# Retention state of the prompt multiplied between the output projection and the gate product, in a one-layer hybrid decoder on one core

## The chip, the cores and the metric

One core of a Trainium2 chip runs the whole step as one program. The time is what the device needs for one execution, in microseconds (us); the median of several executions is given, with the lowest and the highest beside it. The profile is of one further execution. Its engines are named as in its rows: PE is TensorE's matmuls and PEld its weight loads, DVE is VectorE, ACT is ScalarE, POOL is GpSimd, SP is SyncE, which only issues DMAs here.

## What is computed

A decoder layer with two kinds of mixer heads (SSD and retention) and a SwiGLU feed-forward part, on 264 columns that matter at the end: 256 prompt tokens and 8 sample tokens (16 meta tokens run ahead of the prompt, so 272 prompt columns pass through the mixers). Cut to what the change touches:

```python
h = h + rmsnorm(mix @ w_out, post_mix_g)          # the kernel's stage "o" and its norm
f = rmsnorm(h, pre_ffn_g)                         # the second norm of the same h
f = (silu(f @ w_gate) * (f @ w_up)) @ w_down      # stages "f" and "d"
h = h + rmsnorm(f, post_ffn_g)
# two of the states of the prompt that are outputs too:
ret_state  = sum over tokens j of  gamma**(271 - j) * outer(k_j, v_j)      # per head, 256 x 256, 4 heads
ssm_state  = sum over tokens j of  w_j * outer(x_j * dt_j, B_j)            # per group
```

The two state sums need nothing of `w_out` or of the feed-forward part: their operands (`ktok`, `vtok`; `xdt`, `btok`) are there long before, and nothing reads them but the stores to the outputs.

## The kernel before

All activations lie transposed: 128 features on the partitions, the tokens along the free axis. A matrix of 2048 rows is 16 k-tiles. Weights are not resident: `Stream` (line 110) walks through all weight blocks in the order of use, eight 128x128 blocks to a chunk of 512 KB. Each chunk is loaded by SP into `raw` (four buffers), cast by ScalarE to a rounded copy `hi` (line 123) and subtracted by VectorE to the remainder `lo` (line 124); `hi` and `lo` have three buffers each. Every 128x128 block then takes three matmuls (`three`, lines 132 to 134): `hi` by the rounded activation, `hi` by its remainder, `lo` by the rounded activation. An activation is split in the same manner by `split` (line 653): ScalarE writes the rounded half (line 654), VectorE the remainder (line 655).

`gemm` (line 136) goes through output tiles one after the other, each with all its k-tiles, and evicts each tile from its PSUM bank. With `outer=n` the first n output tiles run k-outer: for each k-tile all n tiles are advanced, so that the product can begin when the first k-tile of its input is there. For stage `f` (gate and up, 88 output tiles) this holds for the first six (OUTF = 6): 16 k-tiles x 6 tiles x 3 = 288 matmuls, which use 12 chunks of weights. Their first four banks are of the pool `pg` (4 banks, tag `g`), the other two of `pm` (4 banks, tag `m`), in which the norm's sums (`n30`, `n40`), the banks of the state products (`ps0` to `ps7`, `hs0`, `hs1`) are allocated too.

Between stage `o` and stage `f` lies the double norm (lines 777 to 802). `rstds` multiplies the sums of squares by ones on TensorE and takes Ln and Exp on ScalarE (lines 645, 647). Then, for each of the 16 k-tiles: VectorE multiplies by `rstd` (line 788) and adds the residual `xr` (line 789), `split` makes `fh` and `fl` (ScalarE, then VectorE), ScalarE squares the tile into `hq` (line 792), and GpSimd adds that to a running sum `hs` (line 797). The residual comes in pairs of tiles, by DMAs that GpSimd issues (line 786) into three buffers of the pool `sd`; the result is stored for later, four tiles at a time, into `hd` (line 802), also from GpSimd's queue. The second norm's factor `rhc` is wanted only when the first six tiles of `f` are evicted: `ffn_norm` (line 806) runs after the k-outer part of `gemm`, before its evictions (line 859).

`do_pret` (line 619) is the retention state: for each of 8 (head, half) tiles three matmuls of 256 columns into a bank, a copy by ScalarE (`pso`, line 628) and a store issued by GpSimd. `PRE = 1`: head 0 stands behind the norm's loop, heads 1 to 3 after the first six tiles of `f`, followed by `do_pssm` (line 430), which weighs `xdt` on VectorE (line 432) and multiplies it into `hs0` and `hs1`.

The order on each engine is fixed when the program is built: a planner takes, for each engine, the first ready instruction in program order, with some moved up: the chunk casts by 1500 places, an eviction's first reading by 3000. Tiles of one pool and tag are handed buffers; the pool `sp` (tag `s`) has 27 slots of 128x1120 words, in which `o`, `mh`, `ml`, `fh`, `fl`, `ktok`, `vtok`, `xdt`, `btok` and later `ah`, `al` lie.

Of the kernel before, what the change touches and what calls it, by code (L numbers as in the profile page):

```python
# [7 lines left out]
F32 = mybir.dt.float32  # L8
F32R = mybir.dt.float32r
AF = mybir.ActivationFunctionType  # L10
# [5 lines left out]
P = 128  # L16
DM = 2048
KT = DM // P
NMETA = 16
NPR = 272  # L20
NA = 280
NO = 264
# [24 lines left out]
DECAY_ACT = False  # L47
WARM = 9
OUTF = 6
PRE = 1  # L50


@with_exitstack
def hybrid_step(ctx: ExitStack, tc: tile.TileContext, wall, xT, pp, cc, dmask, cs, convst, ssm, ret,
                yT, oconv, opssm, opret, osssm, osret):
    nc = tc.nc
    V, A, G, T = nc.vector, nc.scalar, nc.gpsimd, nc.tensor
    MULT, ADD, SUB, MAX, MIN = ALU.mult, ALU.add, ALU.subtract, ALU.max, ALU.min

    cp = ctx.enter_context(tc.tile_pool(name="cp", bufs=1))  # L60
    st = ctx.enter_context(tc.tile_pool(name="st", bufs=3))
    sp = ctx.enter_context(tc.tile_pool(name="sp", bufs=NSLOT))
    ta = ctx.enter_context(tc.tile_pool(name="ta", bufs=9))
    sd = ctx.enter_context(tc.tile_pool(name="sd", bufs=3))
# [6 lines left out]
    def slot(name, w=NA, n=4, dt=F32):  # L71
        return sp.tile([P, n, w], dt, name=name, tag="s")

    def small(name, w=NA):
        t = ta.tile([P, 308], F32, name=name, tag="t")
        return t[:, :w]

    def bank(name, w=512):
        t = pm.tile([P, 512], F32, name=name, tag="m")
        return t[:, :w]  # L80

    def table(name):
        return tc.keep_in_program_order(A.preload_act_table_set(name))

    def load(out, in_):
        G.dma_start(out, in_)
# [6 lines left out]
    def par(n, i=0, w=1):  # L93
        return pps[:, PP[n][0] + i:PP[n][0] + i + w]
# [41 lines left out]
    def gemm(name, xin, nk, n, m0, m1, evict, outer=0, pool=pg, before=None):  # L136
        off = 0
        if outer:
            pss = [pg.tile([P, 512], F32, name=f"{name}{m}", tag="g") if m < m0 + 4 else
                   pm.tile([P, 512], F32, name=f"{name}{m}", tag="m") for m in range(m0, m0 + outer)]  # L140
            for k in range(nk):
                xh, xl = xin(k, n)
                for ps in pss:
                    three(ps[:, :n], xh, xl, k == 0, k == nk - 1)
            if before:
                before()
            for m in range(m0, m0 + outer):
                evict(m, pss[m - m0][:, :n])
            m0 += outer
        for m in range(m0, m1):  # L150
            ps = pool.tile([P, 512], F32, name=f"{name}{m}", tag="g" if pool is pg else "m")
            for k in range(nk):
                xh, xl = xin(k, n)
                three(ps[:, :n], xh, xl, k == 0, k == nk - 1)
            evict(m, ps[:, :n])
# [271 lines left out]
                                   ps, MULT, ADD)  # L427
            yield

    def do_pssm():  # L430
        for b in range(3):
            V.tensor_tensor(xdt[b], xdt[b], wj[:, b, :].unsqueeze(2).to_broadcast([P, 16, 64]), MULT)
        for g in range(2):
            ps = bank(f"hs{g}")
            for b in range(3):
                T.matmul(ps, btok[:, b, g * P:(g + 1) * P], xdt[b][:, 8 * g:8 * g + 8, :].rearrange("p h d -> p (h d)"),
                         start=(b == 0), stop=(b == 2))
            for f in (0, 256):
                t = small(f"hso{g}{f}", 256)
                A.copy(t, ps[:, f:f + 256])  # L440
                load(opssm[:, g * 512 + f:g * 512 + f + 256], t)
# [177 lines left out]
    def do_pret(h0, h1):  # L619
        for h in range(h0, h1):  # L620
            for t in range(2):
                m = 2 * h + t
                ps = bank(f"ps{m}", 256)
                for b in range(3):
                    T.matmul(ps, ktok[b][:, m, :], vtok[b][:, 2 * h:2 * h + 2, :].rearrange("p a d -> p (a d)"),
                             start=(b == 0), stop=(b == 2))
                o = small(f"pso{m}", 256)
                A.copy(o, ps)
                load(opret[:, m, :], o)


    def rstds(name, groups, scale, outs=None, load_table=True):
        pss = []
        for g, sums in enumerate(groups):
            ps = bank(f"{name}{g}", NO)
            for i, s in enumerate(sums):
                T.matmul(ps, ones, s, start=(i == 0), stop=(i == len(sums) - 1))
            pss.append(ps)
        if load_table:
            table("natural_log_exp_and_others")  # L640
        rs = outs or [small(f"{name}r{g}", NO) for g in range(len(groups))]
        sc = scale if isinstance(scale, list) else [scale] * len(groups)
        with tc.high_priority(offset=1000):
            for ps, r, c in zip(pss, rs, sc):
                A.activation(r, ps, AF.Ln, bias=eps, scale=c)
            for r in rs:
                A.activation(r, r, AF.Exp, scale=-0.5)
        return rs
# [4 lines left out]
    def split(hi, lo, src, scale):  # L653
        A.activation(hi, src, AF.Copy, scale=scale)  # L654
        V.scalar_tensor_tensor(lo, src, scale, hi.bitcast(F32), MULT, SUB)
# [98 lines left out]
    def ev_norm(o, gain):  # L754
        st_ = {}

        def ev(m, ps):
            i, j = divmod(m, 4)
            sq = small(f"{gain}q{m}", NO)
            with tc.high_priority(offset=3000):  # L760
                A.activation(sq, ps, AF.Square)
                V.tensor_scalar(o[i][:, j, :], ps, par(gain, m), None, MULT)
            if m == 0:
                st_["a"] = sq
            elif m < KT - 1:
                n = small(f"{gain}s{m}", NO)
                G.tensor_tensor(n, st_["a"], sq, ADD)
                st_["a"] = n
            else:
                st_["b"] = sq  # L770
        return ev, st_

    o = [slot(f"o{i}", NO) for i in range(4)]
    ev, sums = ev_norm(o, "g_post")
    table("natural_log_exp_and_others")
    gemm("o", min_, KT, NO, 0, KT, ev, outer=4)
# [1 line left out]
    hd = dp.tile([P, KT, NO], F32, name="hd")  # L778
    fh = [slot(f"fh{i}", NO, dt=F32R) for i in range(4)]
    fl = [slot(f"fl{i}", NO, dt=F32R) for i in range(4)]  # L780
    ha = None
    for k in range(KT):
        i, j = divmod(k, 4)
        if k % 2 == 0:
            xr = sd.tile([P, 2, NO], F32, name=f"xr{k}", tag="st")
            load(xr, xT[:, k:k + 2, NMETA:NA])
        ok = o[i][:, j, :]
        V.tensor_tensor(ok, ok, rstd, MULT)
        V.tensor_tensor(ok, ok, xr[:, k % 2, :], ADD)
        split(fh[i][:, j, :], fl[i][:, j, :], ok, par("g_ffn", k))  # L790
        sq = small(f"hq{k}", NO)
        A.activation(sq, ok, AF.Square)
        if k == 0:
            ha = sq
        elif k < KT - 1:
            n = small(f"hs{k}", NO)
            G.tensor_tensor(n, ha, sq, ADD)
            ha = n
        else:
            hb = sq  # L800
        if j == 3:
            load(hd[:, 4 * i:4 * i + 4, :], o[i])
    do_pret(0, PRE)
    rhc = cp.tile([P, NO], F32, name="rhc")

    def ffn_norm():
        rstds("n4", [[ha, hb]], 1.0 / DM, [rhc], False)


    mix.close()  # L810
# [44 lines left out]
    def ev_f(m2, ps):  # L855
# [12 lines left out]
        if m < 41 and (m + 1) * 25 // 41 > n:  # L868
            pace = ta.tile([P, 1], F32, name=f"pace{m}", tag="pace", bufs=2)
            tc.keep_in_program_order(G.tensor_copy(pace, t[:, 0:1]))  # L870
            state_step(n)

    gemm("f", fin, KT, NO, 0, OUTF, ev_f, outer=OUTF, before=ffn_norm)
    do_pret(PRE, 4)
    do_pssm()
    gemm("f", fin, KT, NO, OUTF, 2 * FT, ev_f)

# [22 lines left out]
    for n in range(8):  # L900
        ok = o2[n // 2][:, 2 * (n % 2):2 * (n % 2) + 2, :]
# [116 lines left out]
```

## Time and profile before

| | us |
|---|---|
| median of 3 runs | 1285.83 |
| lowest to highest | 1283.55 to 1287.29 |
| the profiled execution | 1283.67 |
| its span, first to last instruction | 1281.8 |

| stage | stretch of the span, us |
|---|---|
| norm, mixers and their projections | 0 to 379 |
| `o`: the output projection | 379 to 472.2 |
| double norm, then the six k-outer tiles of `f` | 472.2 to 516.8 |
| rest of the state products | 517 to 531.4 |
| rest of `f` | 531.4 to 1007 |
| `d`: the down projection | 1007 to 1264 |
| last norm and output | 1264 to 1281.8 |

Matmuls are pipelined: a row's duration of 0.28 us is that from start to end, and the next one starts 0.12 us after it. A loss on TensorE is therefore read from start to start. A wide fp32 matmul (the state products, the sums by ones) shows as two instructions.

### The profile page before, as it was taken

The numbers are of one execution on the slowest core, as the hardware profiler recorded it, in microseconds if no ns is written. First come the engines' busy times: TensorE is split into PE (matmuls) and PEld (weight loads), VectorE is DVE, ScalarE is ACT, GpSimd is POOL, SyncE is SP. The second block draws the span as 40 slices with busy tenths as digits, with TensorE's granted clock in tenths as the row PEclk, the third lists the DMA queues.
The fourth block names the chain that finished last, engine by engine and source line by source line (L and its number), as shares of the span: only waits on it lengthen the run. The fifth ranks groups of instructions, "written<-read, shape, count | busy, mean of one in ns | idle before, by whom it ended". The sixth has DMA issues, their size and how long they took to land.

```text
span 1281.8 us, 24583 instructions
## 1 busy us (share of the span) xinstructions
PE 1255.2 (98%) x10078; PEld 1240.1 (97%) x10078; DVE 825.6 (64%) x1259; ACT 608.0 (47%) x838; POOL 170.0 (13%) x236
## 2 busy tenths in 40 slices
PE   8999999999999999999999999999999999999994
PEld 7999999999999998899999999999999999999994
DVE  7978879884774459466666666666666544444445
ACT  6665344455854446444444444444444433333331
POOL 3320001110001225201110110101101000000013
PEclk9999999999999999999999999999999999999997
DMA  7566448774455556577677777766676555555562
GB/s 271 206 202 203 140 143 286 280 262 120 163 195 181 181 173 231 183 247 234 230 243 246 237 229 241 247 215 246 214 246 230 181 181 181 181 182 181 181 223 93
DMA packets 74832, 266.41 MB, mean 208 GB/s; under 512 B 8592, under 2 KB 9504, under 8 KB 74720
## 3 DMA queue, kind: packets, MB, share of 16 engines
q1 hardware_dynamic: 60192, 214.17, 50.9%
q0 software_dynamic: 13808, 49.52, 10.7%
q8 instruction: 79, 1.29, 0.4%
q10 hardware_dynamic: 720, 1.16, 0.2%
q14 instruction: 33, 0.27, 0.1%
HBM read 246.15 MB, written 18.66 MB: 207 GB/s over the span
## 4 chain that ended last, share of the span: by engine, by line
PE 93%; DVE 3%; DMA 1%; issue 1%; ACT 1%; SPq 0%; POOL 0%; DVEq 0%; ACTq 0%
PE f L132 13%; PE f L133 13%; PE f L134 13%; PE d L133 7%; PE d L132 7%; PE d L134 7%; PE o L132 2%; PE o L133 2%; PE o L134 2%; PE xb L133 1%; PE xb L134 1%; PE xb L132 1%; PE k L132 1%; PE v L132 1%; PE v L133 1%; PE k L133 1%
## 5 line engine op out<-in xcount | busy, mean ns | idle before, releaser
L124 DVE TENSOR_TENSOR lo<-raw,hi 128x1024 fp32r<-128x1024 f32 (+1 forms) x405 | 493.1, 1219 | 360.0 <-ACT hi L123 354.9
L123 ACT CAST hi<-raw 128x1024 fp32r<-128x1024 f32 (+1 forms) x405 | 421.8, 1042 | 587.9 <-PE f L133 183.0
L134 PE MATMUL f<-fh,lo 128*128 128x264 f32 x1408 | 398.6, 283 | 2.7 <-DVE lo L124 2.6
L132 PE MATMUL f<-fh,hi 128*128 128x264 f32 x1408 | 399.9, 284 | 1.0 <-ACT fh L654 1.0
L133 PE MATMUL f<-fl,hi 128*128 128x264 f32 x1408 | 400.0, 284 | 0.0
L134 PEld LDWEIGHTS f<-fh,lo 128*128 128x128 f32 x1408 | 265.1, 188 | 3.7 <-DVE lo L124 3.7
L132 PEld LDWEIGHTS f<-fh,hi 128*128 128x128 f32 x1408 | 264.4, 188 | 1.7 <-ACT fh L654 1.4
L133 PEld LDWEIGHTS f<-fl,hi 128*128 128x128 f32 x1408 | 264.4, 188 | 0.5 <-issue 0.2
L133 PE MATMUL d<-al,hi 128*128 128x264 f32 x704 | 199.9, 284 | 0.0
L134 PE MATMUL d<-ah,lo 128*128 128x264 f32 x704 | 199.8, 284 | 0.0
L132 PE MATMUL d<-ah,hi 128*128 128x264 f32 x704 | 199.6, 284 | 0.0
L132 PEld LDWEIGHTS d<-ah,hi 128*128 128x128 f32 x704 | 132.6, 188 | 0.0
L133 PEld LDWEIGHTS d<-al,hi 128*128 128x128 f32 x704 | 132.4, 188 | 0.0
L134 PEld LDWEIGHTS d<-ah,lo 128*128 128x128 f32 x704 | 132.2, 188 | 0.0
L870 POOL COPY pace<-f 128x1 f32<-128x1 f32 x25 | 29.2, 1166 | 343.8 <-DVE f L864 343.8
L132 PE MATMUL o<-mh,hi 128*128 128x264 f32 x256 | 72.8, 284 | 0.0
L133 PE MATMUL o<-ml,hi 128*128 128x264 f32 x256 | 72.6, 284 | 0.0
L134 PE MATMUL o<-mh,lo 128*128 128x264 f32 x256 | 72.4, 283 | 0.0
L859 DVE TENSOR_TENSOR f<-f,rhc 128x264 f32<-128x264 f32 x88 | 37.6, 432 | 48.8 <-PE f L134 48.5
L132 PE MATMUL xb<-uh,hi 128*128 128x280 f32 x208 | 61.2, 295 | 3.1 <-ACT hi L123 3.1
L133 PE MATMUL xb<-ul,hi 128*128 128x280 f32 x208 | 61.0, 294 | 1.2 <-DVE ul L172 1.2
L134 PE MATMUL xb<-uh,lo 128*128 128x280 f32 x208 | 60.4, 293 | 0.8 <-DVE lo L124 0.8
(298 smaller groups left out, 2004.7 us busy)
## 6 DMA issues: line engine op xcount, KB each, us to landing
raw<-in_dram SPq DMA_DIRECT2D x401, 512.0 KB, 3.6
rs<-in_dram POOLq DMA_DIRECT2D x16, 512.0 KB, 5.1
su<-in_dram POOLq DMA_DIRECT2D x16, 512.0 KB, 5.0
out_dram<-su POOLq DMA_DIRECT2D x16, 512.0 KB, 4.8
hb<-in_dram POOLq DMA_DIRECT2D x8, 512.0 KB, 5.6
hu<-in_dram POOLq DMA_DIRECT2D x8, 512.0 KB, 5.0
out_dram<-hu POOLq DMA_DIRECT2D x8, 512.0 KB, 4.2
lcb<-lcd POOLq DMA_DIRECT2D x4, 544.0 KB, 7.4
```

The lines of the kernel that those rows point to most:

```text
L123: A.copy(self.hi[:, f:f + w], raw[:, f:f + w])
L124: V.tensor_tensor(self.lo[:, f:f + w], raw[:, f:f + w], self.hi[:, f:f + w].bitcast(F32), SUB)
L132: T.matmul(ps, hi, xhi, start=first, stop=False)
L133: T.matmul(ps, hi, xlo, start=False, stop=False)
L134: T.matmul(ps, lo, xhi, start=False, stop=last)
L859: V.tensor_tensor(t, ps, rhc, MULT)
L870: tc.keep_in_program_order(G.tensor_copy(pace, t[:, 0:1]))
```

## The change

`do_pret` for all four heads is called inside the double norm's loop, one head (two banks, six matmuls) after each of the first four pairs of tiles; the constant PRE goes away, and nothing of `do_pret` is left behind the first six tiles of `f`. The loop goes by pairs of tiles: one multiplication and one addition on 128x2x264 elements, while the split stays tile by tile. The residual is loaded into four slots of `sp` of four tiles each, in program order ahead of the output projection. The squares are taken four tiles at a time, into the residual's slot, and summed by VectorE after the loop, down to two tiles of 264 columns; GpSimd adds nothing in this norm. The weighing of `xdt` (three multiplications) becomes a function of its own, called behind these sums and ahead of stage `f`.

```diff
-PRE = 1
...
-    def do_pssm():
+    def weigh_xdt():
         for b in range(3):
             V.tensor_tensor(xdt[b], xdt[b], wj[:, b, :].unsqueeze(2).to_broadcast([P, 16, 64]), MULT)
+
+    def do_pssm():
         for g in range(2):
...
     o = [slot(f"o{i}", NO) for i in range(4)]
+    xr = []
+    for i in range(4):
+        xr.append(slot(f"xr{i}", NO))
+        load(xr[i], xT[:, 4 * i:4 * i + 4, NMETA:NA])
     ev, sums = ev_norm(o, "g_post")
...
-    ha = None
-    for k in range(KT):
+    for k in range(0, KT, 2):
         i, j = divmod(k, 4)
-        if k % 2 == 0:
-            xr = sd.tile([P, 2, NO], F32, name=f"xr{k}", tag="st")
-            load(xr, xT[:, k:k + 2, NMETA:NA])
-        ok = o[i][:, j, :]
-        V.tensor_tensor(ok, ok, rstd, MULT)
-        V.tensor_tensor(ok, ok, xr[:, k % 2, :], ADD)
-        split(fh[i][:, j, :], fl[i][:, j, :], ok, par("g_ffn", k))
-        sq = small(f"hq{k}", NO)
-        A.activation(sq, ok, AF.Square)
-        if k == 0:
-            ha = sq
-        elif k < KT - 1:
-            n = small(f"hs{k}", NO)
-            G.tensor_tensor(n, ha, sq, ADD)
-            ha = n
-        else:
-            hb = sq
-        if j == 3:
+        ok = o[i][:, j:j + 2, :]
+        V.tensor_tensor(ok, ok, rstd.unsqueeze(1).to_broadcast([P, 2, NO]), MULT)
+        V.tensor_tensor(ok, ok, xr[i][:, j:j + 2, :], ADD)
+        for q in (j, j + 1):
+            split(fh[i][:, q, :], fl[i][:, q, :], o[i][:, q, :], par("g_ffn", 4 * i + q))
+        if k < 8:
+            do_pret(k // 2, k // 2 + 1)
+        if j == 2:
             load(hd[:, 4 * i:4 * i + 4, :], o[i])
-    do_pret(0, PRE)
+            A.activation(xr[i], o[i], AF.Square)
+    hsum = xr[0]
+    for i in range(1, 4):
+        V.tensor_tensor(hsum, hsum, xr[i], ADD)
+    V.tensor_tensor(hsum[:, 0:2, :], hsum[:, 0:2, :], hsum[:, 2:4, :], ADD)
+    weigh_xdt()
     rhc = cp.tile([P, NO], F32, name="rhc")
 
     def ffn_norm():
-        rstds("n4", [[ha, hb]], 1.0 / DM, [rhc], False)
+        rstds("n4", [[hsum[:, 0, :], hsum[:, 1, :]]], 1.0 / DM, [rhc], False)
...
     gemm("f", fin, KT, NO, 0, OUTF, ev_f, outer=OUTF, before=ffn_norm)
-    do_pret(PRE, 4)
     do_pssm()
```

## Rows read from the trace of the kernel before

**Rows 1.** The page's busy time, share of the span and instructions of each engine.

```profile
PE 1255.2 (98%) x10078; PEld 1240.1 (97%) x10078; DVE 825.6 (64%) x1259; ACT 608.0 (47%) x838; POOL 170.0 (13%) x236
```

**Rows 2.** Stretches: length, busy PE, PEld, DVE, ACT, POOL; granted clock, DMA share, GB/s.

```profile
379.00:472.00 93.00, 93.00 (x769) 92.86 (x768) 46.82 (x50) 40.02 (x50) 18.99 (x14) 1.00 0.54 181
472.00:532.00 60.00, 56.32 (x373) 49.99 (x372) 45.48 (x74) 34.40 (x69) 25.59 (x35) 1.00 0.65 213
...
512.00:517.00 5.00, 5.00 (x42) 4.97 (x41) 2.38 (x2) 1.30 (x2) 0.00 (x0) 1.00 0.95 318
```

**Rows 3.** Waits, 472 to 532: engine, line, releaser; total us, times, longest.

```profile
PEld f L134 <- DVE lo L124: 3.7, 5, 1.5
...
PE f L132 <- ACT fh L654: 1.0, 1, 1.0
```

**Rows 4.** Chain that ended last, 470 to 533: start, us, engine, tile, line.

```profile
516.83 0.89 PE n L637 x4
517.72 2.59 PE ps L625 x12
521.04 5.22 PE ps L625 x24
526.25 5.15 PE hs L436 x12
```

**Rows 5.** Timeline around 477 us, PE: start, us, engine, line, operation, [idle before].

```profile
477.12 0.87 PE L132 MATMUL f<-fh,hi 128*128 128x264 f32 x5 [1.00 <-ACT fh L654]
```

**Rows 6.** Timeline of DVE and of POOL, 478 to 482.

```profile
478.62 1.00 DVE L655 SCALAR_TENSOR_TENSOR fl<-o,pps,fh 128x264 fp32r<-128x264 f32 x1
...
481.13 0.48 DVE L655 SCALAR_TENSOR_TENSOR fl<-o,pps,fh 128x264 fp32r<-128x264 f32 x1
...
478.19 1.13 POOL L797 TENSOR_TENSOR hs<-hq,hq 128x264 f32<-128x264 f32 x1 [0.31 <-ACT hq L792]
...
480.82 0.57 POOL L86 DMA_DIRECT2D hd<-o  x1 [0.59 <-DVE o L789]
```

**Rows 7.** Groups by shape, 470 to 520: count | busy us, mean ns | idle before.

```profile
L124 DVE TENSOR_TENSOR lo<-raw,hi 128x1024 fp32r<-128x1024 f32 x14 | 17.9, 1284 | 6.8 <-ACT hi L123 6.8
...
L655 DVE SCALAR_TENSOR_TENSOR fl<-o,pps,fh 128x264 fp32r<-128x264 f32 x16 | 12.9, 831 | 0.0
L797 POOL TENSOR_TENSOR hs<-hs,hq 128x264 f32<-128x264 f32 x13 | 12.4, 957 | 4.2 <-ACT hq L792 3.6
L654 ACT ACTIVATE fh<-o,pps 128x264 fp32r<-128x264 f32 x16 | 8.0, 511 | 13.2 <-DVE o L789 13.2
L789 DVE TENSOR_TENSOR o<-o,xr 128x264 f32<-128x264 f32 x16 | 7.6, 494 | 0.0
L788 DVE TENSOR_TENSOR o<-o,n3r 128x264 f32<-128x264 f32 x16 | 6.9, 458 | 0.4 <-ACT n3r L647 0.4
...
L625 PEld LDWEIGHTS ps<-vtok,ktok 128*128 128x128 f32 x24 | 4.6, 190 | 0.7
...
L628 ACT COPY pso<-ps 128x256 f32<-128x256 f32 x2 | 0.6, 368 | 0.0
```

**Rows 8.** Instructions of single tiles: ns least/median/most, first to last start.

```profile
L788 DVE TENSOR_TENSOR o<-o,n3r x16: 419/421/982, 475.4 to 505.9; 128x264 f32<-128x264 f32 x16
...
L655 DVE SCALAR_TENSOR_TENSOR fl<-o,pps,fh x16: 480/977/1547, 477.1 to 508.8; 128x264 fp32r<-128x264 f32 x16
...
L897 DVE TENSOR_TENSOR p<-p,n5r x7: 694/1795/1803, 1266.3 to 1276.7; 128x528 f32<-128x528 f32 x7
...
L432 DVE TENSOR_TENSOR xdt<-xdt,wj x3: 1216/1217/1220, 176.6 to 180.3; 128x1024 f32<-128x1024 f32 x3
```

**Rows 9.** Timeline of DVE, evictions of the first six tiles of f.

```profile
518.97 2.12 DVE L859 TENSOR_TENSOR f<-f,rhc 128x264 f32<-128x264 f32 x6
```

**Rows 10.** Timeline around 1217 us: VectorE's, then GpSimd's queue.

```profile
1216.69 0.48 DVE L762 TENSOR_SCALAR p<-d,pps 128x264 f32<-128x264 f32 x1
...
1217.33 0.58 POOL L86 DMA_DIRECT2D hr<-hd  x1
```

## The prediction

> **What bounds the kernel now.** TensorE is busy for 1255.2 of the span's 1281.8 us [rows 1], so the time falls only by what TensorE stops losing between its first and its last matmul. I read four views, in this order. The table of stretches shows where it loses anything: the output projection runs without a hole (93.00 of 93.00), the 60 us behind it do not (56.32) [rows 2]; the change touches little else. The granted clock is 1.00 in both, so nothing there is lost to a slow clock. The waits of those 60 us name the cause: the gate product's matmuls and weight loads waited for VectorE's remainders `lo` and, once, for ScalarE's first `fh` [rows 3]. The chain that ended last and two rows of the timeline give the times. And the groups by shape show why VectorE was late.
>
> The loss itself, from start to start. In the output projection 769 matmuls take 93.00 us, 0.121 each [rows 2]. The 288 matmuls of the six k-outer tiles should thus take 34.8, and 0.16 more until the last has left the array: 35.0. They run from 477.12 [rows 5] to 516.83, where the norm's sums follow [rows 4]: 39.7. So 4.7 are lost inside the gate product's first tiles, and 1.0 ahead of its first matmul [rows 5]: **5.7 us**. All else on TensorE up to the last matmul of the state products (531.40 [rows 4]) is work that stays.
>
> The Trainium skill ("Perfetto Trace Analysis", Identifying the Most-Contended Engine) would have TensorE's headroom judged by the busy share of the weight loads, not of the matmuls. Weight loads are busy for 49.99 of the 60 [rows 2], so by that measure 10.0 would be to be had and the time would be 1275.8. The trace agrees only once the state products are taken out: their 48 loads of 190 ns [rows 7] lie 0.2175 apart, their matmuls being that long, and the twelve of `hs` 0.43 apart [rows 4], which hides 1.3 + 2.9 us of loads that could not be denser.
>
> **Why VectorE was late.** From 475.4 to 509 it goes without a pause through the norm's 16 tiles and the casts of the weight chunks. Many of its instructions ran far above their own least. The remainder `fl` takes 480 ns at least and 831 in the mean; multiplication and addition 419 at least, 458 and 494 in the mean; the cast 1284 against 1217 for an addition of its shape [rows 7, 8]. Over 16, 16, 16 and 14 of them that is 5.6 + 0.6 + 1.2 + 0.9 = 8.3 us. What they met is GpSimd's running sum: the `fl` at 478.62 lay beside one and took 1.00; the one at 481.13 lay beside a store's issue from GpSimd and took 0.48 [rows 6]. So it is the additions, not the DMA issues, that slow VectorE.
>
> **The change, part by part.**
>
> *GpSimd's sums go; pairs.* The 8.3 us of disturbance go with the 14 additions. A multiplication of 128x528 takes 694 ns undisturbed [rows 8], against twice 419: eight pairs of two such instructions save 2.3. VectorE's own load for the six tiles becomes 16 x 0.694 + 16 x 0.480 + 12 casts x 1.217 = 33.4 us. Added are its sums: three additions of 1056 elements, 1.25 each scaled from the 1024 of [rows 8], and one of 528: 4.5. Together 37.9; begun at 475.4 as now, they end at 513.3.
>
> *State products into the norm.* The 36 instructions moved take 2.59 + 5.22 = 7.8 us [rows 4], as much in front of the gate product as behind it. TensorE is out of such work at 476.1 now (477.12 less the 1.0 idle) and would go on to 483.9. The pair's first `fh` is ready long before: 475.4 + 2 x 0.69 + 0.51 = 477.3 (it is later by the pair, which costs nothing under this cover). So the 1.0 goes.
>
> *Does TensorE then ever catch up with VectorE?* In the 8.5 us of head start VectorE makes, at 2.35 per pair (two of 0.694, two of 0.480), 3.6 pairs, seven of the 16 k-tiles. TensorE needs 18 x 0.121 = 2.18 per k-tile; VectorE makes one in 1.17, plus 0.91 for the three quarters of a chunk that it uses: 2.09. It starts seven ahead and is the faster one. So the 4.7 go as well. The gate product ends at 483.9 + 35.0 = 518.9, the sums of squares are ready 5.6 before that, and with 0.89 for the norm and 5.15 for `hs` [rows 4] the next tile begins at 524.9. Before, `hs` ended at 531.4 with 0.7 of that tile already done (the gap from 520.31 to 521.04): 530.7. Difference 5.8, the 5.7 above but for rounding.
>
> *Banks.* New is that the third to eighth state products wait for PSUM banks. Four serve the norm's sum, the products and two of the six gate tiles, and each comes free by a ScalarE copy (0.37 [rows 7]) that stands behind the `fh` of its pair. If they are handed out in program order, the fifth gate tile needs the copy behind the sixth `fh`: three pairs of VectorE's two wide steps and two of its remainders, 475.4 + 4.2 + 1.9, then two `fh` of 0.51 and the copy: 482.9. TensorE comes there at 483.9. It fits by 1.0; a chunk's cast or two of 1.2 ahead of a pair would make it late by 0.2 to 1.4. Bounds 0 and 1.4; I take 0.4, nearer to zero because the casts have three buffers full at that time.
>
> *Evictions of the six tiles.* They lose 7.8 us of cover. The first `f` eviction began 2.1 after the norm's matmul and the six took 2.12 [rows 4, 9]; the next tile needs the first bank only 0.89 + 5.15 = 6.0 after that matmul. Cost nothing, with 3.5 to spare.
>
> *At nothing, too.* The residual's loads: buffers seem to be handed out in program order, for the reload `hr` goes out 0.64 after the first write to the fourth tile of `p` [rows 10], so `xr` should go out once the fourth tile of `o` is begun, its 13th of 16 columns, three columns of 48 x 0.121 ahead of the end: 17 us before the norm. If one came late, the 8.5 us of products cover it. The squares: at most as long as now, ScalarE waits 13.2 us in this norm [rows 7]. The eight stores and their copies: GpSimd has lost 13.5 us of sums, and its issues do not disturb VectorE. The weighing of `xdt` runs at 176.6 to 181 already [rows 8], ready long before its place in the program, and nothing new holds it back.
>
> Sum: -1.0 - 4.7 + 0.4 = **-5.3 us**. The profiled execution took 1283.67, its span and 1.9 around it; it would become 1278.4. It lies 2.2 under the median of the runs shown, and from that median 1285.8 - 5.3 = **1280.5**.
>
> **The rivals.**
>
> *Half of it.* Casts go ahead of pairs in VectorE's order; one that waits for a buffer which TensorE frees only in the gate product holds up all pairs behind it, and with them copies, banks and the fifth gate tile. For it: VectorE waited 6.8 us for casts in this stretch [rows 7]. Against: such a wait begins only when three chunks are full. At two casts and one such wait, 2.4 + 0.5 of the gain: 1283.4.
>
> *It does not move.* The planner leaves the products behind the gate product, as it may where banks are short. Then only the disturbance goes: VectorE at 2.09 per k-tile against 2.18, without a head start; 1.0 + 0.6 (the wider pair) at the front stay lost, 4.1 comes: 1281.7 at best, nearer to 1283 with stalls at each cast.
>
> *Given back behind the tiles.* The gate product is no longer starved, but the norm of its evictions is late by as much, TensorE's queue being in order: 1285.8.
>
> *Slower: the tail of VectorE's queue.* The sums now stand on VectorE alone, and TensorE's norm matmul stands in front of `hs` and of the next tile's banks. If the four additions and the weighing (3 x 1.217, no longer early) come behind the casts for the chunks after the sixth tile, which need buffers freed at the very end (one copy and one cast, 2.3 after the gate product's end), `hs` could start only 2.3 + 4.5 + 3.65 = 10.4 after it instead of 0.9: 9.5 lost against 5.7 won, 1289.6. It turns the change to a loss as soon as `hs` starts later than 6.6 after the gate product's end. Against it: VectorE is busy for only 2.38 of the 5 us up to 517 [rows 2], and the weighing ran at 176.
>
> **How the numbers follow.** This kernel's runs can tell some 0.3% (3.9 us) from no change. Forecast: 0.60 (1279.9 to 1281.4). Half: 0.17. Does not move: 0.06. Given back: 0.09. Slower: 0.08, of it 0.07 beyond 0.3%. Faster by over 0.3%, that is under 1282.0, takes most of the forecast and a little of the third case: 0.62; within: 0.31; slower: 0.07. The runs of before lie 2.3 below and 1.5 above their median, so the range goes from 1278.0, two under the forecast, to 1286.0, the given-back case; outside it lie the slower case and the ends of the scatter.
>
> **What would show it.** In the changed profile: `ps` of all eight banks between the output projection and the first gate matmul, with TensorE idle there under 0.5; 288 gate matmuls in some 35 us; `fl` at 480 in the mean; the sums' last addition before the sixth tile's end; `hs` at once behind the norm's matmuls; `xdt` weighed near 176. I am wrong if the waits for `lo` come back, if TensorE waits for a bank among the `ps`, or if the norm's matmul waits for VectorE.

## The result, and the profile after

| | before | after |
|---|---|---|
| median, us | 1286.28 (10 runs) | 1280.24 (10 runs) |
| lowest to highest | 1283.39 to 1289.31 | 1276.15 to 1282.03 |
| ratio, 95% interval | | 0.995 (0.9938 to 0.9961) |
| profiled execution, and its span | 1283.67, 1281.8 | 1281.7, 1279.9 |
| first `k` matmul to the end of the span | 1185.7 | 1179.8 |
| lost between the norm's sums and the end of `hs` | 5.6 | 0.0 |

The kernel is faster by 6.0 us of the medians. The two profiled spans differ by only 1.9. The first matmul of the stage `k`, far ahead of the change, shows why. TensorE's timeline (start, duration, engine, line, operation, operands), before:

```profile
96.07 0.29 PE L132 MATMUL k<-uh,hi 128*128 128x280 f32 x1
```

and after:

```profile
100.08 0.30 PE L131 MATMUL k<-uh,hi 128*128 128x280 f32 x1
```

The profiled execution of after happened to reach `k` 4.0 later. From there to the end it takes 5.9 less. This start of `k` differs from run to run in both kernels; the last experiment is about what it hangs on. Wherever two profiles are compared below, two numbers are given that it does not touch: the **span from `k` on**, and the **loss**. The loss is the time from the first matmul of the first norm's sums, which stand behind the output projection, to the end of the last one of `hs`, less the 0.73 us of gate work that lies inside where state products stand behind the gate product, and less 52.75, which is what the changed kernel takes. Before, the sums begin here (chain that ended last: start, duration, what):

```profile
472.37 0.45 PE n L637 x2
```

and `hs` ends at 531.40 [rows 4], so the loss is 59.03 - 0.73 - 52.75 = 5.6. (That the span from `k` on falls by 0.3 more than the loss was not followed.)

That 52.75 holds no hole. The page's busy times of after:

```profile
PE 1254.4 (98%) x10078; PEld 1240.9 (97%) x10078; DVE 821.3 (64%) x1247; ACT 607.8 (47%) x826; POOL 153.1 (12%) x218
```

and one stretch (length, busy PE, PEld, DVE, ACT, POOL, granted clock, DMA share, GB/s), cut at the times of [rows 2] although the sums begin 4.0 later here:

```profile
472.00:532.00 60.00, 60.00 (x418) 55.28 (x417) 43.17 (x65) 34.49 (x59) 10.91 (x19) 1.00 0.61 203
```

Over the whole span the shares say nearly nothing: TensorE 98% in both [rows 1], VectorE 821.3 after 825.6. In the one stretch that matters TensorE has gone from 56.32 of 60 to 60.00 [rows 2], and GpSimd's busy time from 25.59 to 10.91. PEld is still idle for 4.72 there with TensorE full, close to the 4.2 that the prediction put down to the wide state products; so the weight loads' share would still promise headroom where none is left.

The chain of work that ended last, after (start, duration, what):

```profile
476.39 0.45 PE n L638 x2
476.83 0.86 PE ps L626 x4
477.70 0.71 PE n L638 x2
478.40 9.50 PE ps L626 x44
...
523.10 0.89 PE n L638 x4
523.99 5.15 PE hs L437 x12
```

All 48 instructions of the state products lie ahead of the gate product and end at 487.90; the norm's sums begin at 523.10, 35.2 later (39.7 before), and `hs` stands right behind them. No wait of TensorE for `lo` or `fh` is left among the waits of this stretch [rows 3].

The groups by shape from 470 to 525, after (busy, mean ns of one, idle before them and what ended it), answer to [rows 7]:

```profile
L123 DVE TENSOR_TENSOR lo<-raw,hi 128x1024 fp32r<-128x1024 f32 x15 | 18.3, 1222 | 15.3 <-ACT hi L122 15.3
...
L656 DVE SCALAR_TENSOR_TENSOR fl<-o,pps,fh 128x264 fp32r<-128x264 f32 x16 | 7.3, 487 | 0.0
L789 DVE TENSOR_TENSOR o<-o,n3r 128x528 f32<-128x528 f32 x8 | 5.5, 702 | 0.6 <-ACT n3r L648 0.6
L790 DVE TENSOR_TENSOR o<-o,xr 128x528 f32<-128x528 f32 x8 | 5.5, 701 | 0.0
...
L800 DVE TENSOR_TENSOR xr<-xr,xr 128x1056 f32<-128x1056 f32 x3 | 3.8, 1251 | 0.0
```

The remainder `fl` has fallen from 831 to 487 ns in the mean, the cast `lo` from 1284 to 1222, each to within 2% of the least value forecast for it, and VectorE now waits for casts: 15.3 us here, and 11.9 from 474 to 524, which is the stretch of [rows 7] moved by the 4.0, where before it waited 6.8. It is the engine that stands idle. The pairs' steps take 0.70, the wide sums 1.25, as forecast.

Three rows of the timeline show where details came out otherwise (ScalarE, VectorE and GpSimd, after):

```profile
478.93 0.37 ACT L629 COPY pso<-ps 128x256 f32<-128x256 f32 x1
...
505.38 0.70 DVE L801 TENSOR_TENSOR xr<-xr 128x528 f32<-128x528 f32 x1
...
525.23 2.12 DVE L858 TENSOR_TENSOR f<-f,rhc 128x264 f32<-128x264 f32 x6
...
379.03 3.01 POOL L85 DMA_DIRECT2D xr<-in_dram  x4 [106.04 <-PE g L133]
```

The first bank's copy was put ahead of the first `fh` (481.64). The fifth copy, which frees the fifth gate tile's bank, ended at 485.14, behind the fourth `fh` where the prediction had counted on the sixth; TensorE came to that tile at 489.2. The last sum of squares was done at 506.1, 17 us ahead of its use. The evictions began 2.13 after the norm's first matmul, as forecast. And the residual was loaded at 379, its issue having waited for the last `g` matmul, whose operands held the slots; not 17 us ahead of the norm.

### The profile page after: what moved, and what is told of

The parts are those of the page before. It is cut to its first block, busy times and chain, and to the rows that moved or that the text cites. A ratio compares the mean times of both kernels' runs of the same rounds, so it can differ in the third digit from the quotient of the medians.

```text
span 1279.9 us, 24519 instructions
## 1 busy us (share of the span) xinstructions
PE 1254.4 (98%) x10078; PEld 1240.9 (97%) x10078; DVE 821.3 (64%) x1247; ACT 607.8 (47%) x826; POOL 153.1 (12%) x218
## 4 chain that ended last, share of the span: by engine, by line
PE 95%; DMA 2%; DVE 1%; issue 1%; SPq 0%; ACT 0%; POOL 0%; DVEq 0%; ACTq 0%
PE f L131 13%; PE f L133 13%; PE f L132 13%; PE d L132 7%; PE d L131 7%; PE d L133 7%; PE o L131 2%; PE o L132 2%; PE o L133 2%; PE xb L132 1%; PE xb L133 1%; PE xb L131 1%; PE k L131 1%; PE v L131 1%; PE v L132 1%; PE k L132 1%
## 5 line engine op out<-in xcount | busy, mean ns | idle before, releaser
L123 DVE TENSOR_TENSOR lo<-raw,hi 128x1024 fp32r<-128x1024 f32 (+1 forms) x405 | 492.3, 1217 | 357.8 <-ACT hi L122 353.1
```

Of the source, the lines that this page charges most:

```text
L123: V.tensor_tensor(self.lo[:, f:f + w], raw[:, f:f + w], self.hi[:, f:f + w].bitcast(F32), SUB)
```

## The experiments

Two theories stand against each other at first: that the **place** of the state products did it (TensorE has cover while VectorE works ahead), and that the end of **GpSimd's sums** did it (VectorE no longer disturbed).

| kernel | time, us | loss | span from `k` on |
|---|---|---|---|
| before | 1286.28 | 5.6 | 1185.7 |
| after | 1280.24 | 0.0 | 1179.8 |
| `e1_place`: before, products in the loop | 1286.59 | 7.4 | 1188.0 |
| `e2_norm`: after, products behind as before | 1282.29 | 3.9 | 1183.7 |
| `e3_gpsum`: after, GpSimd's sums back | 1287.61 | 6.5 | 1186.5 |
| `e4_nopair`: after, tile by tile | 1281.11 | 0.0 | 1179.7 |
| `e5_two`: after, two heads in the loop | 1277.49 | 0.2 | 1180.0 |
| `e6_hsfront`: after, `hs` ahead of the gate product | 1280.72 | - | 1182.4 |
| `e10_copies`: `e3_gpsum`, all products ahead of the loop | 1284.03 | 3.9 | 1183.9 |
| `e11_xloop`: after, residual loaded in the loop | 1278.38 | 0.0 | 1180.1 |
| `e13_gplate`: after, four wide sums on GpSimd | 1284.32 | 2.3 | 1182.4 |
| `e8_lct`: after, an early step put elsewhere | 1276.10 | 0.0 | 1179.9 |

The times of `e3_gpsum`, `e4_nopair`, `e5_two`, `e6_hsfront`, `e10_copies`, `e11_xloop` and `e13_gplate` are of one execution each, which carries the scatter of the start of `k`; they are read by the last two columns. These columns come from one trace of each kernel; how far the loss varies between executions of the same kernel is not known. The kernels ran in groups, each beside before: with `e1_place` to `e4_nopair` before took 1285.48 in the median, with `e5_two`, `e6_hsfront`, `e10_copies` and `e8_lct` 1286.88, with `e11_xloop` and `e13_gplate` 1287.18 (one execution).

**The place alone.**

```diff
         split(fh[i][:, j, :], fl[i][:, j, :], ok, par("g_ffn", k))
+        if k % 2 == 1 and k < 8:
+            do_pret(k // 2, k // 2 + 1)
...
-    do_pret(0, PRE)
...
-    do_pret(PRE, 4)
```

> The kernel before with one edit: one head of the retention state behind each of the first four pairs of tiles in the norm's loop, none behind the gate product's first six tiles. GpSimd's sums, single tiles and the residual's loads stay. Loss is counted on TensorE from the end of the output projection's matmuls to the end of hs, against 52.7 us of work there (before 5.6, after 0). Theory A (either cure is enough, and the cover is the stronger one): TensorE starts the gate product 6.8 us later, VectorE has 8.5 us of head start at 1.78 per k-tile without casts, some five tiles, and in the kernel before its last fl came at 508.8 where TensorE would now want it at 516.6; loss 0 to 1, time 5 us under before. Theory B (GpSimd's sums are the cause, cover only hides the 1.0 at the front): loss 4.7, time 1 us under before.

1286.59 against 1285.48 for before on the same chip, ratio 1.0008 (0.9996 to 1.0020): no gain, and the trace loses 7.4 instead of 5.6, more than either theory had said (0 to 1, and 4.7). TensorE's rows that waited, in the timeline of this kernel:

```profile
483.65 2.86 PE L625 MATMUL ps<-vtok,ktok 128*128 128x256 f32 x12 [1.36 <-ACT pso L628]
...
505.44 0.39 PE L134 MATMUL f<-fh,lo 128*128 128x264 f32 x1 [2.92 <-DVE lo L124]
```

and the stretches around the longer wait (columns as above):

```profile
502.00:507.00 5.00, 2.08 (x14) 1.86 (x13) 3.53 (x6) 3.48 (x8) 2.90 (x4) 0.90 0.56 203
507.00:512.00 5.00, 5.00 (x34) 5.00 (x34) 4.15 (x3) 1.73 (x2) 1.90 (x2) 0.76 0.81 230
```

First the products wait for a bank, whose copy on ScalarE is late. Then the gate product waits 2.92 for one cast, and the granted clock falls to 0.90 and 0.76 in the means of the two stretches: for some 3 us the matmuls lie 0.22 apart instead of 0.12, the lower of TensorE's two levels, 1.2 GHz. The chain of this kernel names what the cast was late for:

```profile
496.12 1.08 POOL out_dram L86 x2
...
497.21 0.91 POOL hs L799
498.12 5.25 DMA xr<-in_dram
```

A load of the residual, issued by GpSimd behind its own sums and the products' stores, held VectorE. So the place without the rest is worth nothing: the head start is lost again when VectorE is held up. Two things hold it up here, GpSimd's sums and the late load; `e3_gpsum` and `e11_xloop` take them one at a time. The theory of the place alone falls.

**The norm alone.**

```diff
-        if k < 8:
-            do_pret(k // 2, k // 2 + 1)
...
+    do_pret(0, 1)
...
     gemm("f", fin, KT, NO, 0, OUTF, ev_f, outer=OUTF, before=ffn_norm)
+    do_pret(1, 4)
```

> The changed kernel with the retention state put back where it was: head 0 behind the norm's loop, heads 1 to 3 behind the gate product's first six tiles. Pairs, residual loaded ahead and sums on VectorE stay. Theory A: VectorE at 2.09 us per k-tile just keeps up with TensorE's 2.18 but without a head start; 1.0 + 0.6 at the front stay lost, and perhaps 1 more at casts: loss 1.6 to 2.6, time 3 to 4 under before. Theory B (the sums are the cause): the same, loss 1.6. Theory C (only the cover counts): loss as before, 5 to 6, no gain.

1282.29 against 1285.48, ratio 0.998 (0.9964 to 0.9995): a gain of 3.2 by the medians, with 0.6 to 4.6 in the interval. In the profiled execution 3.9 are lost, between the forecasts (1.6 to 2.6, and 5 to 6), none of it to a wait for `lo`. The first gate matmuls in TensorE's timeline:

```profile
483.21 1.47 PE L131 MATMUL f<-fh,hi 128*128 128x264 f32 x5 [2.07 <-ACT fh L655]
484.48 0.42 PE L132 MATMUL f<-fl,hi 128*128 128x264 f32 x1
```

and their stretch:

```profile
482.00:487.00 5.00, 3.79 (x18) 3.79 (x19) 5.00 (x10) 2.71 (x5) 0.94 (x2) 0.66 0.52 203
```

and the norm's sums behind the gate product, in the chain:

```profile
520.17 0.89 PE n L638 x4
```

The wider pair makes the first `fh` later, and with one head of products there is too little work to cover it: 2.07 of wait where before had 1.00 [rows 5]. What follows runs at 0.22 from start to start, granted clock 0.66 in the mean of the stretch. The wait and the slower matmuls behind it, which make the gate product 37.0 long instead of 35.2, come to about the 3.9. By the medians the loss would be 2.4 (5.6 less the gain of 3.2). The profiled execution (1286.48) was one of the three longest of ten, but its `k` also began latest of all traces, at 101.0, so its length does not say whether 3.9 is much for this kernel. The norm alone with single tiles was not tried; how much of its loss is the pair's stays open.

**GpSimd's sums back**, all else as in the changed kernel.

```diff
+            sq = small(f"hq{m}", NO)
+            A.activation(sq, o[i][:, q, :], AF.Square)
...
+                n = small(f"hs{m}", NO)
+                G.tensor_tensor(n, ha, sq, ADD)
...
-    for i in range(1, 4):
-        V.tensor_tensor(hsum, hsum, xr[i], ADD)
```

> The changed kernel with the squares taken tile by tile and summed by GpSimd again; placement, pairs and residual ahead stay. Theory A: fl goes back to over 0.7 us in the mean, but the head start hides it: TensorE's loss stays under 0.5. Theory B: the waits for lo come back, loss 3 to 4.

The loss is 6.5, more than before's 5.6 and more than either theory had said (under 0.5, and 3 to 4). `fl` is back, and TensorE's worst wait is of a new kind. The group by shape of this kernel:

```profile
L656 DVE SCALAR_TENSOR_TENSOR fl<-o,pps,fh 128x264 fp32r<-128x264 f32 x16 | 11.3, 736 | 0.0
```

the timeline, TensorE and then ScalarE:

```profile
492.33 0.59 PE L131 MATMUL f<-fh,hi 128*128 128x264 f32 x1 [3.18 <-ACT pso L629]
492.72 0.42 PE L132 MATMUL f<-fl,hi 128*128 128x264 f32 x1
...
489.41 0.52 ACT L655 ACTIVATE fh<-o,pps 128x264 fp32r<-128x264 f32 x1 [3.20 <-DVE o L790]
...
491.93 0.62 ACT L629 COPY pso<-ps 128x256 f32<-128x256 f32 x2
```

and the stretches:

```profile
487.00:492.00 5.00, 2.15 (x12) 1.73 (x10) 5.00 (x8) 2.13 (x6) 3.29 (x4) 0.96 0.40 156
492.00:497.00 5.00, 4.67 (x21) 4.67 (x22) 5.00 (x7) 3.12 (x9) 3.40 (x5) 0.50 0.28 104
```

The gate product waits for a bank. The copy that frees it stands behind `fh` in ScalarE's fixed order, and that `fh` waited 3.20 for VectorE's addition. This is the bank wait that the prediction had priced at 0.4: it is 3.18 once VectorE is late, and the granted clock is 0.50 in the stretch behind it, 28 matmuls at 0.22 apiece, some 2.7 us more. So with the products in the new place the sums decide everything: 0 without them, 6.5 with them. (The edit also takes the squares tile by tile on ScalarE again; `e13_gplate` moves additions alone.)

**Is it only the banks?** If `e3_gpsum` lost its time to the bank alone, all products ahead of the loop, with their copies ahead of every `fh`, would give it back. Against `e3_gpsum`:

```diff
     fl = [slot(f"fl{i}", NO, dt=F32R) for i in range(4)]
+    do_pret(0, 4)
     for k in range(0, KT, 2):
...
-        if k < 8:
-            do_pret(k // 2, k // 2 + 1)
```

> The kernel with GpSimd's sums restored (tile-wise squares, all else as changed), and in addition all four heads of the retention state stand ahead of the norm's loop instead of inside it, so that ScalarE's copies that free their banks no longer stand behind the fh of a later pair. GpSimd disturbs VectorE as much as there (fl over 0.7 us in the mean). Theory F (the loss of 6.5 there was the fifth gate tile's bank, held by a copy behind a late fh, and the slow clock after that wait): no wait for pso, clock 1.00, loss under 1. Theory B (the sums starve the gate product of fh, fl and lo whatever the banks do): loss 3 or more, waits for lo.

No wait for a bank is left, yet 3.9 are lost. The timeline of this kernel, VectorE and then TensorE:

```profile
493.00 1.89 DVE L123 TENSOR_TENSOR lo<-raw,hi 128x1024 fp32r<-128x1024 f32 x1
494.81 3.21 DVE L656 SCALAR_TENSOR_TENSOR fl<-o,pps,fh 128x264 fp32r<-128x264 f32 x4
...
499.11 1.21 DVE L123 TENSOR_TENSOR lo<-raw,hi 128x1024 fp32r<-128x1024 f32 x1
...
500.38 0.39 PE L133 MATMUL f<-fh,lo 128*128 128x264 f32 x1 [2.18 <-DVE lo L123]
```

and the stretch behind the wait:

```profile
500.00:505.00 5.00, 4.62 (x25) 4.62 (x26) 5.00 (x6) 3.05 (x7) 4.74 (x6) 0.66 0.66 226
```

Between two casts VectorE has a block of the norm's work, its `fl` at 0.8 each; the second cast comes too late for the gate product by 2.18, and the clock falls again. A head start in k-tiles of the activation does not help here, because only three chunks of weights can be cast ahead. The banks were the first place where VectorE's lateness showed, not its cause.

**Only four additions on GpSimd**, the wide ones.

```diff
     for i in range(1, 4):
-        V.tensor_tensor(hsum, hsum, xr[i], ADD)
-    V.tensor_tensor(hsum[:, 0:2, :], hsum[:, 0:2, :], hsum[:, 2:4, :], ADD)
+        G.tensor_tensor(hsum, hsum, xr[i], ADD)
+    G.tensor_tensor(hsum[:, 0:2, :], hsum[:, 0:2, :], hsum[:, 2:4, :], ADD)
```

> The changed kernel with its four wide additions of squares on GpSimd instead of VectorE; they still run behind the loop, not beside the pairs. If the loss comes from GpSimd's additions running beside the norm's first pairs, and not from GpSimd being slow at them: fl stays at 0.49 us in the mean, the additions take some 3.4 us each from about 500 and end near 512, 10 before they are wanted; TensorE's loss under 0.5. If VectorE had no time to spare once the casts are slowed beside them: waits for lo, loss over 2.

The expectation's premise failed: the additions were not put behind the pairs but beside them, each as its squares were ready. So it does not tell additions beside the pairs from additions behind them. By its numbers the second theory came (a wait for `lo`, loss over 2), and it shows what four additions do when they lie beside VectorE's work. The timeline, GpSimd and then VectorE:

```profile
489.31 3.10 POOL L800 TENSOR_TENSOR xr<-xr,xr 128x1056 f32<-128x1056 f32 x1 [0.24 <-ACT xr L797]
...
490.06 2.65 DVE L656 SCALAR_TENSOR_TENSOR fl<-o,pps,fh 128x264 fp32r<-128x264 f32 x1
```

the group by shape:

```profile
L656 DVE SCALAR_TENSOR_TENSOR fl<-o,pps,fh 128x264 fp32r<-128x264 f32 x16 | 11.7, 760 | 0.0
```

and TensorE's longest wait (total, times, longest):

```profile
PE f L133 <- DVE lo L123: 1.7, 1, 1.7
```

An `fl` of 0.48 took 2.65 and ended at 492.71, 0.3 after the addition beside it (492.41). Not every instruction beside it was slowed: VectorE's multiplication at 489.40 took its 0.70, and the addition took 3.10 where the third of its shape took 2.46. Four instructions on GpSimd lift the mean of `fl` to 760 and cost 2.3 us. That is what the Trainium skill ("SBUF — State Buffer", Who interferes with whom) describes: a VectorE instruction with two inputs in SBUF contends with a GpSimd instruction that reads SBUF, and the contention is an exclusive lock. Here the end of `fl`, 0.3 behind the addition's, agrees with it; which of the ports is meant no run shows.

**The other parts of the change**, one at a time: no pairs; two heads in the loop, two behind the gate tiles; the residual loaded in the loop.

```diff
-        V.tensor_tensor(ok, ok, rstd.unsqueeze(1).to_broadcast([P, 2, NO]), MULT)
-        V.tensor_tensor(ok, ok, xr[i][:, j:j + 2, :], ADD)
         for q in (j, j + 1):
+            V.tensor_tensor(o[i][:, q, :], o[i][:, q, :], rstd, MULT)
+            V.tensor_tensor(o[i][:, q, :], o[i][:, q, :], xr[i][:, q, :], ADD)
```

> The changed kernel with multiplication and addition tile by tile again (two of 0.42 in place of one of 0.70); all else stays. VectorE has 2.3 us more to do. Theory A: hidden, loss under 0.3, the first gate matmul where it is now because the state products still lie ahead of it.

```diff
-        if k < 8:
+        if k < 4:
             do_pret(k // 2, k // 2 + 1)
...
+    do_pret(2, 4)
```

> The changed kernel with only heads 0 and 1 of the retention state in the norm's loop, heads 2 and 3 behind the gate product's first six tiles. VectorE undisturbed. 24 instructions of 0.2175 are 5.2 us of cover, 2.6 more than before the change: TensorE would come to the gate product about 2.5 us after the kernel before did, with the first fh there since a second. Theory D (VectorE undisturbed and any cover that reaches past the first fh is enough): loss 0 to 0.5 of the 52.7 us. Theory E (four heads are needed for the head start): loss over 1.5, waits for lo or fl in the gate product.

```diff
-        load(xr[i], xT[:, 4 * i:4 * i + 4, NMETA:NA])
...
-        V.tensor_tensor(ok, ok, xr[i][:, j:j + 2, :], ADD)
+        xr = sd.tile([P, 2, NO], F32, name=f"xr{k}", tag="st")
+        load(xr, xT[:, k:k + 2, NMETA:NA])
+        V.tensor_tensor(ok, ok, xr, ADD)
```

> The changed kernel with the residual loaded as before: eight loads of a pair of tiles inside the norm's loop, into three buffers, issued from GpSimd's queue between the stores of the retention state. Theory G (loading ahead counts: with the products' stores in the loop the loads queue up behind them, as in the kernel with the placement alone, where VectorE waited 1.5 us for one): VectorE waits for xr, loss 1 or more. Theory H (without GpSimd's sums that queue is empty enough: a load lands 3 to 5 us after its issue and stands two pairs ahead): loss under 0.5.

Loss 0.0, 0.2 and 0.0. The pairs save VectorE 2.6 us (multiplication and addition 432 each without them, against 351 a tile with them), which it does not need. Two heads of cover, 4.3 us of it behind the norm's last sum, are enough for a VectorE that nobody disturbs; the head start of seven k-tiles was more than the gate product wants. The residual in the loop does make VectorE wait 1.3, and the cover hides it. Each of these three is worth nothing by itself once the sums are off GpSimd and the cover is there; what they would be worth with the sums there was not tried apart from the first experiment, where the residual's load cost much.

**How much do the evictions need `hs` behind the gate product?**

```diff
     weigh_xdt()
+    do_pssm()
...
-    do_pssm()
```

> The changed kernel with hs multiplied in front of the gate product too, so that nothing covers the norm and the evictions behind the sixth tile. By the prediction's step on the evictions, the next tile's bank comes 2.1 + 0.4 us after the norm's first matmul, which with its three fellows takes 0.9: TensorE idles 1.7 us. If the granted clock stays at 2.4 GHz: loss 1.7. If a wait of that length lets it fall to 1.2 GHz, as the waits of 2.1 and 3.2 us in the two kernels before did: 3 to 4. Were the cover of hs not needed: 0.

TensorE's timeline, the first matmul after the norm's sums:

```profile
527.45 0.39 PE L131 MATMUL f<-fh,hi 128*128 128x264 f32 x1 [1.72 <-DVE f L859]
```

and its stretch:

```profile
525.00:530.00 5.00, 3.28 (x25) 2.83 (x24) 4.17 (x10) 4.65 (x9) 0.15 (x1) 1.00 0.72 208
```

1.72 of wait for the first eviction, 1.6 from the forecast's numbers (2.1 and one eviction of 0.35, less 0.89 for the sums); the span from `k` on is 2.6 longer, between the two forecasts (1.7, and 3 to 4), and what makes up the other 0.9 was not followed. The granted clock stayed at 1.00. So `hs` behind the gate product is work that covers something, while the other 48 instructions cover nothing there.

**The start of `k`.** Both kernels scatter by some 6 us. The waits from 60 to 110 of the changed kernel (engine, line, releaser; total, times, longest):

```profile
DVE wj L304 <- DMA lcb<-lcd: 6.2, 2, 3.9
...
PE xb L133 <- DVE lo L123: 3.4, 1, 3.4
```

and a stretch of it:

```profile
90.00:95.00 5.00, 2.49 (x12) 2.50 (x13) 3.80 (x8) 4.58 (x8) 0.56 (x3) 0.79 0.33 90
```

VectorE stands in line for a load that lands 6.6 to 11.7 us after its issue, the casts queue behind it, and TensorE waits 3.4. Over this profile and ten others TensorE's wait is 0.7 to 3.9. The step that waits (`wj`) is called between two tiles of `xb`; the experiment calls it two tiles later:

```diff
-        if 7 <= m < 10:
+        if m in (7, 8, 11):
             next(held["dt"])
```

> The changed kernel with one more edit far ahead of the change: the transposes behind which wj and the first decay masks stand come two output tiles later (third step at tile 11 instead of 9), while the four broadcast loads lcb go out as early as now. Aimed at what the profiles differ in from run to run: the first matmul of k starts at 96.1 to 101.0 us, because VectorE stands in line for lcb and TensorE waits 0.8 to 3.9 for lo behind it, the clock going down to 0.6 to 0.8 in the longer cases. Theory: no wait for lcb on VectorE, k starts near 95 in every run, 4 us faster than the changed kernel and the runs within 2 us of one another instead of 6. Rival: the loads land when they land and the masks are wanted at once for k: the wait moves to tile 12 and the time stays.

1276.10 (1275.67 to 1276.28, four runs) against 1286.88 for before on that chip, ratio 0.9912 (0.9896 to 0.9929), and a scatter of 0.6. The same wait:

```profile
DVE wj L304 <- DMA lcb<-lcd: 0.8, 1, 0.8
```

and the same stretch:

```profile
90.00:95.00 5.00, 5.00 (x41) 5.00 (x40) 4.18 (x15) 3.25 (x6) 0.00 (x0) 1.00 0.72 279
```

No wait of TensorE for `lo` is left there, and `k` begins at 94.44. The load still takes 6.2 to 11.5 to land; VectorE's wait behind it is down to 0.8. This kernel is faster than both, by 4 to 5 us than the changed one (4.1 by the medians, which were not taken side by side, 4.9 by the two ratios to before), and the span from `k` on is the same (1179.9): the two gains have nothing to do with each other.

## Why the prediction was right

- **The sum and the sign.** Forecast -5.3 and 1280.5; measured -6.0 by the medians and 1280.24, -5.9 by the span from `k` on. The loss named (5.7) was there (5.6) and went whole. That the two times agree to 0.3 is luck in part: the median of before that it started from moved by 0.45 with more runs (1285.83 to 1286.28), and the runs of either kernel lie 5.9 apart.
- **GpSimd's sums disturb VectorE** (8.3 us). `fl` fell to 487 and rose again to 736 and 760 when additions came back. Taking the sums off is needed: with them the products in the new place lose 7.4 (`e1_place`) and 6.5 (`e3_gpsum`). It is not enough: without the cover 3.9 are lost in the trace of `e2_norm`. The gain comes of the two together.
- **The products as cover, and the head start.** They came as described, TensorE's idle time ahead of the gate product is gone, and the gate product takes 35.2 (35.0 forecast). The reasoning was needed in sign but not in size: two heads do, and with a late VectorE four do not. The step counted k-tiles of the activation and treated the casts as an even share of VectorE's time; `e10_copies` shows that a cast standing behind a block of the norm's work decides, with three chunks of margin.
- **Banks, +0.4.** The term that was mis-sized: it measured 0. The copies went further ahead than the program order that had been assumed, and the fifth came 4.1 before its bank was wanted, not 1.0. With a late VectorE the same step gives 3.18.
- **VectorE's load, 37.9, done at 513.3.** Its instructions cost what was forecast, 0.70, 0.48, 1.22 and 1.25, but the sums ended 17 us ahead of their use, not 5.6: only five casts lay ahead of them and not twelve, the others waiting for buffers that TensorE frees as it goes. The slower rival, a tail of VectorE's queue, lost its ground by this.
- **Evictions.** 2.13 after the sums' first matmul (2.1 forecast), no wait; `e6_hsfront` shows the cover's worth.
- **The residual's loads.** Wrong in its place, issued at 379 when `g`'s operands let go of the slots, not behind the fourth tile of `o`; harmless, and `e11_xloop` shows that even late loads would have been covered.
- **The weighing** ran at 180.6 to 184.3, early as forecast.
- **The rivals.** "It does not move" had put its loss at 1.6 for the front and the rest, 4.1 of gain. The kernel that is just that, `e2_norm`, lost 3.9 in its profile and gained 3.2 by its medians. Waits were added up there; the slow clock behind them, 1.8 us of the profile's 3.9, was not. "Half of it" needed a cast that holds up the pairs: VectorE's first wait for one comes at 506.5, behind the last pair.
- Not foreseen is the profiles' own scatter: of the two spans' difference, 1.9, a reader would have concluded that two thirds of the forecast had failed.

## What to carry to other kernels

Where VectorE feeds TensorE through a short ring of buffers, GpSimd should do no two-input additions in that stretch: here four of them cost 2.3 us and fourteen 6.5, while a remainder beside a DMA issue took its usual 0.48 [rows 6]. Filler work ahead of a starved product helped here only where the engine that starves it was undisturbed: with the sums on GpSimd a late VectorE first showed as a bank that came late (3.18), and with the banks free as a late cast (2.18). And before two profiles are compared, find the point from which they do the same work, and read the difference from there.

## What was not expected of the hardware

One long wait of TensorE can cost more than its own length. The waits seen, and the mean granted clock of a stretch of the profile that begins at the wait or behind it:

| kernel | wait, us | granted clock behind it |
|---|---|---|
| after, ahead of `k` | 3.4 | 0.79 |
| `e3_gpsum` | 3.18 | 0.50 |
| `e1_place` | 2.92 | 0.76 |
| `e10_copies`, ahead of `k` | 2.56 | 0.66 |
| `e1_place`, ahead of `k` | 2.52 | 1.00 |
| `e10_copies` | 2.18 | 0.66 |
| `e2_norm` | 2.07 | 0.66 |
| `e11_xloop`, ahead of `k` | 2.06 | 1.00 |
| `e6_hsfront` | 1.72 | 1.00 |
| `e13_gplate` | 1.7 | 1.00 |
| before, the longest of several | 1.3 | 1.00 |

Where the clock fell, the matmuls then lie 0.22 apart for a while (0.23 for the wider ones ahead of `k`; the lower level, 1.2 GHz), elsewhere 0.12 or 0.13 (2.4 GHz). The length of the wait alone does not decide it. Ahead of `k` two kernels do the same work and wait for the same cast, `e1_place` (timeline, then stretch):

```profile
90.97 0.40 PE L134 MATMUL xb<-uh,lo 128*128 128x280 f32 x1 [2.52 <-DVE lo L124]
...
90.00:95.00 5.00, 4.03 (x31) 4.04 (x32) 4.92 (x9) 4.95 (x8) 0.56 (x3) 1.00 0.48 135
```

and `e10_copies`:

```profile
90.89 0.40 PE L133 MATMUL xb<-uh,lo 128*128 128x280 f32 x1 [2.56 <-DVE lo L123]
...
90.00:95.00 5.00, 4.11 (x20) 4.11 (x21) 4.92 (x9) 4.94 (x9) 0.55 (x3) 0.66 0.59 159
```

The waits are equal to 0.04; one keeps the clock, the other loses it. What else decides is open, and with it whether the same kernel pays for its wait in every execution.

Before lost its 5.6 in pieces that left the clock alone, the longest in its waits from 472 to 532:

```profile
PE f L134 <- DVE lo L124: 2.6, 3, 1.3
```

The same lateness of VectorE, gathered into one wait by more cover in front of it, can cost nearly twice its length (3.18 and some 2.7 behind it in `e3_gpsum`). That is how the traces of `e1_place` and `e3_gpsum` come to lose more than before.
